# A decoder layer on one core: the second gate's modulation beside the output projection, and nine instead of seven FFN units with seven products

## The chip, the core and the metric

The kernel runs on one core of a Trainium2 chip. It is one program for one transformer layer. The metric is the device time of a whole execution in microseconds (us), as the median of several runs. The engines are named as in the profile: TensorE (PE) for matmuls, VectorE (DVE), ScalarE (ACT), GpSimd (POOL), and SyncE (SP), which here does nothing but issue DMAs. Each engine executes its own list of instructions in a fixed order and waits on semaphores for the others.

## What is computed

One layer over 256 rows (`x` is 1 x 256 x 2048, f32), with six modulation vectors made from a conditioning vector `c`:

```python
mod = silu(c) @ w_ada + b_ada
shift1, scale1, gate1, shift2, scale2, gate2 = split(mod, 6)
h = rms_norm(x, norm1_gain) * (1 + scale1) + shift1
x = x + gate1 * mixing_sublayer(h, ...)        # ends in "y @ w_out"
h = rms_norm(x, norm2_gain) * (1 + scale2) + shift2
x = x + gate2 * swiglu(h, w_ffn_in, w_ffn_out) # (silu(h@Wg) * (h@Wu)) @ w_ffn_out
```

`mixing_sublayer` is one projection `h @ w_in` whose columns feed three token mixers (stick-breaking attention, dilated attention, gated linear attention); their gated sum `y` is projected by `w_out` (2048 x 2048). The FFN is 5632 wide: `w_ffn_in` is 2048 x 11264, `w_ffn_out` 5632 x 2048. `w_ada` is 2048 x 12288, of which each of the six vectors takes 2048 columns.

## The kernel before

**Tiles.** The 256 rows are two tiles t of 128 (NT = 2). The 2048 rows of a weight are 16 chunks k of 128 (KC = 16), its columns are taken in blocks of 512 (NB). Every f32 product is made of three matmuls of a reduced f32 type (`mm3`, L164 to L166): high part by high part, low part of the weight by the high part of the data, high part of the weight by the low part of the data. A block of 512 columns is therefore 16 chunks x 2 tiles x 3 matmuls = 96 matmuls of 128 x 512.

**Weights.** `load_weights` fetches two chunks at a time, a "raw" of 512 KB, with a DMA from SP (L146). ScalarE casts a raw to its high part `whi` (L158), VectorE subtracts to get the low part `wlo` (L159); this is called a split below. A raw is 128 x 1024, the two chunks side by side. There are four rooms each for raw, whi and wlo, and some blocks take spare rooms besides. A raw is fetched when its room is free, so a split that is done late makes a DMA late.

**Stages.** The projections by `w_in` and the mixers run from 0 to about 760 us. Then comes the output projection, four blocks n = 0 to 3. `residual` (L1176, L1177) multiplies a block by gate1 and adds it to x, and ScalarE sums the squares. The last block is done for t = 0 first and for t = 1 afterwards from the same split weights, which stay in eight spare rooms, so that norm 2 of t = 0 runs beside the matmuls of t = 1.

**Norm 2.** `norm2_rows` waits for the sums of squares (L1183), works out the root and scales the 4 x 512 columns of a tile into `ada` (L1187, VectorE). `norm2_turn` transposes these 16 times on TensorE (L1199); ScalarE applies scale2 and shift2 to each 128 x 128 (L1206) and casts the high part H (L1210); VectorE makes the low part (L1211). FFN unit 0 is also done for t = 0 first; the second turn stands within its block for t = 0.

**FFN.** There are 11 units of 512 columns, each with a block for the gate half and one for the up half, then a turn of 8 transposes (L1122) into the layout of the output product. In the units listed in `FAST` three of the eight weight pairs are done by `fast_products` with seven products instead of eight, for which VectorE makes sums of weights (L1296 to L1326). The output product by `w_ffn_out` follows in two halves (`OUT_A`, `OUT_B`).

**Background.** The modulation vectors are made by background generators kept in `bg`. `tick(rate)`, called once for each weight pair of a block, lets them go on by that many steps. A step is a DMA of 512 KB of `w_ada` by SP into one of the rooms in `ring["tags"]` (L384), and, a few steps later, a multiply-and-add of 128 x 1024 on VectorE (L289), a "mac" below. `flush()` does all that remains. gate2 is made in units 8 to 10 and flushed in the output product.

**Order.** A scheduler sets the order of instructions on each engine when the program is built; `prio()` brings work forward, `issue_after` holds a DMA back until a given matmul. Buffers have tags (`A7`, `OS1`, `KD`...): two tiles with the same tag share one piece of memory, and the later one waits for the earlier one's readers.

Of the kernel before, what the change touches and what calls it, by code (L numbers as in the profile page):

```python
# [32 lines left out]
RATE_IN, RATE_MID, RATE_FFN = 0.8, 0.6, 0.65  # L33
RATE_OUT = 2.5
# [10 lines left out]
FAST = range(1, 8)  # L45
# [30 lines left out]
def trunk(ctx: ExitStack, tc: tile.TileContext, I, out):  # L76
# [91 lines left out]
    def block(pss, act, src, k0, k1, c0, base=0, w=None, tiles=range(NT), go_on=False, more=False, seeded=False,  # L168
              steps=None):
# [1022 lines left out]
    def norm2_turn(t, xs):  # L1192
# [8 lines left out]
        for j, ps in enumerate(banks):  # L1201
            hf = S(("KC", "T6")[j - 2], [P, 4, P]) if t == 0 and j >= 2 else scr([P, 4, P])
# [36 lines left out]
    w = load_weights(I["w_out"], 0, KC, 3 * NB, spare=("T0", "T3", "OS0", "OS1", "OS2", "OD", "A7", "A11"))  # L1239
    flush()  # L1240
    sh2, sc2 = mod2[SEG_SHIFT2], mod2[SEG_SCALE2]
    h2 = ([S(f"H{j}", [P, 4, T], F32R) for j in range(4)], [S(f"H{4 + j}", [P, 4, T], F32R) for j in range(4)])
    for t in range(NT):
        ps = acc_bank()
        block({t: ps}, y_at, None, 0, KC, 0, w=w, tiles=(t,), steps={N2_AT[0]: lambda: norm2_turn(0, xs)} if t else None)
# [5 lines left out]
    def h2_at(k, t):  # L1251
# [5 lines left out]
    ftags = ["A0", "A1", "A5", "A6", "A7", "A9", "A10", "A11", "A12", "T0", "T1", "T2", "T3", "T4", "T5",  # L1257
             "OS0", "OS1", "OS2", "OD", "KD", "H0", "H1"]
# [134 lines left out]
    def fast_unit(i):  # L1393
        own, other = (misc_bank, acc_bank) if i % 2 else (acc_bank, misc_bank)
        return fast_products(w_ff, i * NB, DFF + i * NB, PAIRS, h2_at, h2s, own, other, ("OD", "KD"))

    state["rate"] = RATE_FFN
    state["more_rooms"] = tuple(zip(X2_TAGS[0::2], X2_TAGS[1::2]))
    ring["tags"] = ("AR0", "AR1", "KC")
    act = []  # L1400
    for i in range(NFF):
        if i in FAST:
# [3 lines left out]
        if i == FAST[-1] + 1:  # L1406
            ring["tags"] = ("AR0", "AR1", "KC", "A2", "A3")
            bg.append(gate2_bg())
        if i in FAST:
            pass  # L1410
        elif i == 0:
            w = load_weights(w_ff, 0, KC, 0, spare=("A12", "KD", "A9", "A10", "A0", "A1", "T1", "T2"))
            for t in range(NT):
                block(pg, h2_at, None, 0, KC, 0, w=w, tiles=(t,), steps=None if t else {N2_AT[1]: lambda: norm2_turn(1, xs)})
# [150 lines left out]
```

## Time and profile before

| what | value |
|---|---|
| median of 3 runs | 1591.57 us (1590.14 to 1591.96) |
| profiled execution, its own time | 1590.96 us |
| its span, first to last instruction | 1589.2 us |
| PE busy | 1577.6 us (99%) |
| DVE busy | 1299.3 us (82%) |
| ACT busy | 852.6 us (54%) |
| data moved by DMA | 400.16 MB, mean 252 GB/s |
| granted TensorE clock, mean | 1.000 |

The span is 1.8 us shorter than the execution, which includes the start and end. A row of the timeline reads: start in us, duration in us, engine, line, operation, output <- input, shape, and, where the engine stood idle before, the length of that idle time and what ended it. Matmuls are pipelined: a 128 x 512 matmul is listed with 0.39 us, but the next one begins about 0.23 us after it, and it is this distance that counts. A row of the chain of waits gives start, duration and what it is. A row of the windows gives, for a stretch of time, each engine's busy time in us, the granted clock, the DMA share and the rate.

### The profile page before, as it was taken

The page shows a single profiled execution, that of the slowest core. Times are in us where ns is not written, and L with a number is a line of the kernel's source. Part 1 is how long each engine was busy: PE and PEld are TensorE (multiplying, and loading weights), DVE is VectorE, ACT ScalarE, POOL GpSimd, SP SyncE. Part 2 cuts the span into 40 slices and gives each one's busy share as a digit, 9 for nine tenths or more (in the row PEclk, how much of TensorE's full clock was granted, in tenths as well). Part 3 has the DMA queues.
Part 4 walks back from the last instruction along what each step waited for, and adds up shares of the span by engine and source line. Part 5 has one row for each costly group of instructions (what it writes and reads, how often), then busy time and mean ns, then how long its engine had stood idle before and what let it go on. Part 6 is the DMA issues. An engine that isn't in the chain of part 4 may idle for free.

```text
span 1589.2 us, 20174 instructions
## 1 busy us (share of the span) xinstructions
PE 1577.6 (99%) x7243; PEld 1304.6 (82%) x7243; DVE 1299.3 (82%) x1556; ACT 852.6 (54%) x1195; POOL 11.2 (1%) x22
## 2 busy tenths in 40 slices
PE   9999999999999999999999999999999999999998
PEld 7878888888888888888887888888888888888887
DVE  6889996888888686877756689999997677998884
ACT  5654448775764444444445756555554434455552
POOL 1000000000000000000000000000000000000000
PEclk9999999999999999999999999999999999999999
DMA  9999997677788899988767566666668789866664
GB/s 334 360 328 322 333 305 241 212 229 231 231 267 271 300 300 324 307 278 298 230 206 244 174 195 189 198 202 196 206 191 279 259 290 311 275 193 219 201 207 138
DMA packets 195740, 400.16 MB, mean 252 GB/s; under 512 B 13038, under 2 KB 28052, under 8 KB 195640
## 3 DMA queue, kind: packets, MB, share of 16 engines
q1 hardware_dynamic: 194664, 396.70, 75.9%
q0 software_dynamic: 800, 2.11, 0.3%
q8 instruction: 57, 0.93, 0.2%
q14 instruction: 43, 0.35, 0.1%
q10 hardware_dynamic: 176, 0.07, 0.0%
HBM read 394.63 MB, written 4.19 MB: 251 GB/s over the span
## 4 chain that ended last, share of the span: by engine, by line
PE 88%; DVE 4%; ACT 3%; DMA 3%; issue 2%; SPq 0%; ACTq 0%; DVEq 0%
PE acc L166 22%; PE acc L165 21%; PE acc L164 21%; PE misc L165 6%; PE misc L166 6%; PE misc L164 5%; DMA raw<-w_in 2%; PE acc L443 1%; ACT whi L158 1%; DVE wlo L159 1%; DMA raw<-w_br_gla 1%; DVE wlo L1309 1%; PE misc L812 1%; PE misc L1122 1%; ACT scr L638 1%
## 5 line engine op out<-in xcount | busy, mean ns | idle before, releaser
L158 ACT CAST whi<-raw 128x1024 fp32r<-128x1024 f32 x362 | 368.5, 1022 | 406.0 <-PE acc L166 270.2
L159 DVE TENSOR_TENSOR wlo<-raw,whi 128x1024 fp32r<-128x1024 f32 x362 | 425.6, 1183 | 186.8 <-ACT whi L158 184.8
L164 PE MATMUL acc<-whi,H 128*128 128x512 f32 x1245 | 487.3, 392 | 1.2 <-ACT H L455 0.8
L165 PE MATMUL acc<-wlo,H 128*128 128x512 f32 x1245 | 486.3, 391 | 0.8 <-DVE wlo L159 0.7
L166 PE MATMUL acc<-whi,H 128*128 128x512 f32 x1245 | 486.0, 391 | 0.4 <-DVE H L462 0.4
L166 PEld LDWEIGHTS acc<-whi,H 128*128 128x128 f32 x1245 | 233.6, 188 | 50.7 <-DVE H L462 1.6
L164 PEld LDWEIGHTS acc<-whi,H 128*128 128x128 f32 x1245 | 233.7, 188 | 50.0 <-ACT H L455 1.3
L165 PEld LDWEIGHTS acc<-wlo,H 128*128 128x128 f32 x1245 | 233.9, 188 | 48.6 <-DVE wlo L159 1.7
L1308 ACT CAST whi<-raw 128x1024 fp32r<-128x1024 f32 (+1 forms) x148 | 142.0, 974 | 100.4 <-PE acc L166 37.0
L1309 DVE TENSOR_TENSOR wlo<-raw,whi 128x1024 fp32r<-128x1024 f32 (+1 forms) x148 | 162.8, 1122 | 10.9 <-ACT whi L1308 9.5
L165 PE MATMUL acc<-wlo,A 128*128 128x512 f32 x222 | 86.5, 390 | 0.8 <-DVE wlo L159 0.8
L164 PE MATMUL acc<-whi,A 128*128 128x512 f32 x222 | 87.0, 392 | 0.0
L166 PE MATMUL acc<-whi,A 128*128 128x512 f32 x216 | 84.1, 389 | 0.0
L289 DVE SCALAR_TENSOR_TENSOR ada<-AR,csil,ada 128x1024 f32<-128x1024 f32 x51 | 64.8, 1278 | 1.8 <-DMA AR<-w_ada 1.6
L164 PE MATMUL misc<-whi,H 128*128 128x512 f32 x158 | 61.7, 391 | 0.0
L165 PE MATMUL misc<-wlo,H 128*128 128x512 f32 x158 | 61.6, 390 | 0.0
L166 PE MATMUL misc<-whi,H 128*128 128x512 f32 x158 | 61.5, 389 | 0.0
L165 PEld LDWEIGHTS acc<-wlo,A 128*128 128x128 f32 x222 | 41.7, 188 | 9.5 <-DVE wlo L159 1.1
L164 PEld LDWEIGHTS acc<-whi,A 128*128 128x128 f32 x222 | 41.7, 188 | 8.6 <-ACT whi L158 0.3
L1308 ACT CAST A<-raw 128x1024 fp32r<-128x1024 f32 (+1 forms) x36 | 34.9, 982 | 25.5 <-DMA raw<-w_ffn_in 9.1
L1308 ACT CAST whi<-AR 128x1024 fp32r<-128x1024 f32 x24 | 25.3, 1053 | 42.1 <-PE misc L166 20.6
L166 PEld LDWEIGHTS acc<-whi,A 128*128 128x128 f32 x216 | 40.6, 188 | 8.5
(487 smaller groups left out, 2306.3 us busy)
## 6 DMA issues: line engine op xcount, KB each, us to landing
raw<-w_in SPq DMA_DIRECT2D x205, 512.0 KB, 5.0
raw<-w_ffn_in SPq DMA_DIRECT2D x176, 512.0 KB, 4.6
raw<-w_ffn_out SPq DMA_DIRECT2D x88, 512.0 KB, 5.1
AR<-w_ada SPq DMA_DIRECT2D x70, 512.0 KB, 5.0
raw<-w_out SPq DMA_DIRECT2D x32, 512.0 KB, 4.8
KC<-w_ada SPq DMA_DIRECT2D x26, 512.0 KB, 5.3
OS<-w_ada SPq DMA_DIRECT2D x16, 512.0 KB, 6.5
KD<-w_ada SPq DMA_DIRECT2D x16, 512.0 KB, 5.5
```

Of the source, the lines that this page charges most:

```text
L158: state["cast"] = nc.scalar.copy(hi[:, :n, :], raw[:, :n, :])
L159: state["split"] = nc.vector.tensor_tensor(lo[:, :n, :], raw[:, :n, :], hi[:, :n, :].bitcast(F32), op=ALU.subtract)
L164: nc.tensor.matmul(ps, lh, rh, start=start, stop=False, skip_group_check=seeded)
L165: nc.tensor.matmul(ps, lh, rl, start=False, stop=False, skip_group_check=seeded)
L166: state["mm"] = nc.tensor.matmul(ps, ll, rh, start=False, stop=stop, skip_group_check=seeded)
L289: nc.vector.scalar_tensor_tensor(acc, raw, c, acc, op0=ALU.mult, op1=ALU.add)
L443: state["warm"] = nc.tensor.matmul(ps, ones_r, wide, start=True, stop=True)
L638: nc.scalar.activation(junk, heads(b)[:, t, h, :], AF.Square, accum_out=ss[:, t, i : i + 1])
L812: nc.tensor.matmul(ps[:n, t * N_GLA + h, :].rearrange("p (s l) -> p s l", l=L), at(f, h, t)[:, :n], odd(at(f, h, t)), start=True, stop=True,)
L1122: nc.tensor.transpose(ps[:, i, :], src[:, i * P : (i + 1) * P], ident)
L1308: nc.scalar.copy(hi[:, :n, :], src)
L1309: state["split"] = nc.vector.tensor_tensor(lo[:, :n, :], src, hi[:, :n, :].bitcast(F32), op=ALU.subtract)
```

## The change

The change has two parts that share the room for buffers.

*Fast units.* `FAST` is `range(2, 11)` instead of `range(1, 8)`: units 2 to 10 instead of 1 to 7. Unit 1 becomes a plain one, 8, 9 and 10 become fast ones. In unit 10 only one pair of the extra rooms (`more_rooms`) is used.

*Gate2.* Its background generator is started before the output projection instead of in unit 8, at a rate of 0.68 steps for each weight pair, with two accumulators of 128 x 1024 (tags OS0 and T3) and its own rooms for loads (A12, KD, KC, H7, later others). It runs beside the output projection and the first two FFN units, and what is left is flushed ahead of unit 2. `pace` multiplies the rate in the blocks done tile by tile: 0.5 for t = 0 of the last output block, 0 for t = 1 of it, 0 for t = 0 of unit 0 and 0.5 for t = 1. Then GpSimd's queue writes the two sums to DRAM (`gate2_away`), and SP fetches them again in the output product, at hook 7, where `flush` stood. shift2 and scale2 are no longer flushed ahead of norm 2 but ticked until scale2 is there. Some tags change: the spare rooms of the last output block, the places to which x2 is brought back, those of the activations of the last units, and which bank of sums a fast unit starts with.

In all, the changed program has 18 matmuls of 128 x 512 fewer on TensorE, 6 operations of 128 x 1024 and 46 of 128 x 512 more on VectorE, 14 more on ScalarE, and two more DMAs of 128 x 1024 each on POOL and SP.

The order of instructions moves at three places that matter. Lines of the changed kernel are one higher or lower: a split is L158, a mac L290, L1188 is the L1187 of before, L1200 the L1199.

First, SP's queue at the last block of the output projection. Before, its weights stand one after the other, followed by those of FFN unit 0:

```order
L146 DMA raw_7449<-w_out 128x2x512
L146 DMA raw_7455<-w_out 128x2x512
L146 DMA raw_7461<-w_out 128x2x512
L146 DMA raw_7467<-w_out 128x2x512
L146 DMA raw_7473<-w_out 128x2x512
L146 DMA raw_7677<-w_ffn_in 128x2x512
```

Now, with the fourth to eighth raw of the same block (raw_7501 is the fourth) and the steps of gate2:

```order
L145 DMA raw_7501<-w_out 128x2x512
L385 DMA A_1584_7361<-w_ada 128x1024
L385 DMA KD_7388<-w_ada 128x1024
L385 DMA KC_7403<-w_ada 128x1024
L145 DMA raw_7507<-w_out 128x2x512
L385 DMA H_1587_7430<-w_ada 128x1024
L145 DMA raw_7513<-w_out 128x2x512
L385 DMA A_1588_7445<-w_ada 128x1024
L145 DMA raw_7519<-w_out 128x2x512
L145 DMA raw_7525<-w_out 128x2x512
L145 DMA raw_7739<-w_ffn_in 128x2x512
```

Five loads of w_ada have come to stand among the raws; each waits until the mac that read its room last is done, and what is behind it on the queue waits too.

Second, VectorE from the residual of t = 0 in the last block (scr<-T,acc) to the first row of norm 2 (ada). Before:

```order
L1176 TENSOR_TENSOR scr_7536<-T_926_4162,acc_7487 128x512
L1177 TENSOR_TENSOR A_1476_6927<-A_1476_6927,scr_7536 128x512
L159 TENSOR_TENSOR wlo_7680<-raw_7677,whi_7679 128x1024
L1183 TENSOR_REDUCE tiny_7541<-x2ss 128x1
L257 TENSOR_SCALAR tiny_7543<-tiny_7541 128x1
L159 TENSOR_TENSOR wlo_7686<-raw_7683,whi_7685 128x1024
L159 TENSOR_TENSOR wlo_7692<-raw_7689,whi_7691 128x1024
L262 SCALAR_TENSOR_TENSOR tiny_7548<-tiny_7545,tiny_7543 128x1
L263 TENSOR_SCALAR tiny_7548<-tiny_7548 128x1
L159 TENSOR_TENSOR wlo_7698<-raw_7695,whi_7697 128x1024
L1187 TENSOR_SCALAR ada_7551<-A_1473_6921,tiny_7545,tiny_7548 128x512
```

Now, the same stretch, from its residual on:

```order
L1177 TENSOR_TENSOR scr_7598<-T_926_4162,acc_7539 128x512
L290 SCALAR_TENSOR_TENSOR T_1506_6982<-KC_7403,csil,T_1506_6982 128x1024
L1178 TENSOR_TENSOR A_1478_6929<-A_1478_6929,scr_7598 128x512
L158 TENSOR_TENSOR wlo_7748<-raw_7745,whi_7747 128x1024
L1184 TENSOR_REDUCE tiny_7603<-x2ss 128x1
L158 TENSOR_TENSOR wlo_7754<-raw_7751,whi_7753 128x1024
L258 TENSOR_SCALAR tiny_7605<-tiny_7603 128x1
L158 TENSOR_TENSOR wlo_7760<-raw_7757,whi_7759 128x1024
L290 SCALAR_TENSOR_TENSOR OS_1505_6981<-H_1587_7430,csil,OS_1505_6981 128x1024
L263 SCALAR_TENSOR_TENSOR tiny_7610<-tiny_7607,tiny_7605 128x1
L158 TENSOR_TENSOR A_1670_7766<-raw_7763,A_1669_7765 128x1024
L264 TENSOR_SCALAR tiny_7610<-tiny_7610 128x1
```

Behind these come a third mac (T_1506<-A_1588) and then the first L1188: three macs and four splits stand between, where before there were four splits alone.

Third, the two turns of norm 2. TensorE at the first turn, the transposes (misc<-ident,ada) among the matmuls of t = 1 (acc_7556 before). Before:

```order
L164 MATMUL acc_7556<-OS_1593_7469,A_1471_6917 128x512
L1199 MATMUL misc_7587<-ident,ada_7551 128x128 x4
L1199 MATMUL misc_7592<-ident,ada_7551 128x128 x4
L1199 MATMUL misc_7597<-ident,ada_7551 128x128 x4
L1199 MATMUL misc_7602<-ident,ada_7551 128x128 x4
L165 MATMUL acc_7556<-OD_7470,A_1471_6917 128x512
L166 MATMUL acc_7556<-OS_1593_7469,A_1472_6918 128x512
```

Now (acc_7618 is t = 1 of the last block, acc_7737 is unit 0, H its data):

```order
L165 MATMUL acc_7618<-A_1616_7527,A_1472_6918 128x512
L1200 MATMUL misc_7649<-ident,ada_7613 128x128 x4
L1200 MATMUL misc_7654<-ident,ada_7613 128x128 x4
L1200 MATMUL misc_7659<-ident,ada_7613 128x128 x4
L1200 MATMUL misc_7664<-ident,ada_7613 128x128 x4
L163 MATMUL acc_7737<-whi_7741,H_1618_7531 128x512
L164 MATMUL acc_7737<-wlo_7742,H_1618_7531 128x512
```

Before, 37 matmuls of t = 1 stood ahead of the transposes and 11 behind them; now all 48 stand ahead, eight of them among the last of t = 0, and the first product with H follows at once. In the second turn, the six matmuls of t = 0 that stood behind the transposes stand ahead of them too. On VectorE, two macs stand directly ahead of the second turn's L1188, where there was none:

```order
L1212 TENSOR_TENSOR H_1625_7538<-T_1645_7690,H_1621_7534 128x4x128
L158 TENSOR_TENSOR T_1679_7784<-raw_7781,T_1678_7783 128x1024
L263 SCALAR_TENSOR_TENSOR tiny_7727<-tiny_7724,tiny_7722 128x1
L290 SCALAR_TENSOR_TENSOR OS_1505_6981<-KC_7542,csil,OS_1505_6981 128x1024
L264 TENSOR_SCALAR tiny_7727<-tiny_7727 128x1
L290 SCALAR_TENSOR_TENSOR T_1506_6982<-A_1628_7563,csil,T_1506_6982 128x1024
L1188 TENSOR_SCALAR ada_7730<-A_1475_6923,tiny_7724,tiny_7727 128x512
```

The last low part of the first turn (H_1625) still comes ahead of them.

The diff, cut to what the text speaks of:

```diff
-RATE_IN, RATE_MID, RATE_FFN = 0.8, 0.6, 0.65
-RATE_OUT = 2.5
+RATE_IN, RATE_MID, RATE_LATE = 0.8, 0.6, 0.68
-FAST = range(1, 8)
+FAST = range(2, 11)
...
     def block(pss, act, src, k0, k1, c0, ..., steps=None, pace=None):
+        if pace is None:
+            pace = 1.0 if tiles[-1] == NT - 1 else 0.0
         for k in range(k0, k1):
-            if (k - k0) % 2 == 0 and tiles[-1] == NT - 1:
-                tick(state["rate"])
+            if (k - k0) % 2 == 0:
+                tick(state["rate"] * pace)
...
     def bring_back(n):
-        x2[n] = S(X2_TAGS[n], [P, NT, NB])
+        x2[n] = S(("OS1", "OS2", "OD", "KD")[n], [P, NT, NB])
         nc.sync.dma_start(x2[n], x2_away[n])
+    gate2_away = [away.tile([P, 2 * NB], F32, tag=f"gate2_{j}", name=nm("gate2")) for j in range(2)]
+    def gate2_bg():
+        acc = biased([S(tag, [P, 2 * NB]) for tag in ("OS0", "T3")], SEG_GATE2)
+        yield from ada_segment_steps(acc, SEG_GATE2, None, False)
+        yield from last_macs()
+        for j in range(2):
+            nc.gpsimd.dma_start(gate2_away[j], acc[j])
+    state["rate"] = RATE_LATE
+    ring["tags"] = ("A12", "KD", "KC", "H7")
+    bg.append(gate2_bg())
     for n in range(4):
...
-    w = load_weights(I["w_out"], 0, KC, 3 * NB, spare=("T0", "T3", "OS0", "OS1", "OS2", "OD", "A7", "A11"))
-    flush()
+    w = load_weights(I["w_out"], 0, KC, 3 * NB, spare=("T0", "AR0", "AR1", "OS1", "OS2", "OD", "A7", "A11"))
+    ring["tags"] = ("A12", "KD", "KC")
+    while SEG_SCALE2 not in mod2:
+        tick(1)
...
-        block({t: ps}, y_at, None, 0, KC, 0, w=w, tiles=(t,), steps=...)
+        block({t: ps}, y_at, None, 0, KC, 0, w=w, tiles=(t,), steps=..., pace=0 if t else 0.5)
...
-    def gate2_bg():
-        acc = state["gate2"] = biased(halves(S("ada", [P, D])), SEG_GATE2)
-        yield from ada_segment_steps(acc, SEG_GATE2, None, False)
-        yield from last_macs()
...
-    state["rate"] = RATE_FFN
-    ring["tags"] = ("AR0", "AR1", "KC")
+    ring["tags"] = ("A12", "KD", "KC", "T0")
     for i in range(NFF):
+        if i == FAST[0]:
+            flush()
+        if i == NFF - 1:
+            state["more_rooms"] = state["more_rooms"][:1]
...
-        if i == FAST[-1] + 1:
-            ring["tags"] = ("AR0", "AR1", "KC", "A2", "A3")
-            bg.append(gate2_bg())
...
-                block(pg, h2_at, None, 0, KC, 0, w=w, tiles=(t,), steps=...)
+                block(pg, h2_at, None, 0, KC, 0, w=w, tiles=(t,), steps=..., pace=0.5 * t)
...
-    state["rate"] = RATE_OUT
-    hooks[7] = flush
+    def gate2_back():
+        state["gate2"] = [S(tag, [P, 2 * NB]) for tag in ("A2", "A3")]
+        for j in range(2):
+            nc.sync.dma_start(state["gate2"][j], gate2_away[j])
+    hooks[7] = gate2_back
```

More of the change, by code (lines that the diff above doesn't have):

```diff
@@ L1201, in norm2_turn @@
         for j, ps in enumerate(banks):
-            hf = S(("KC", "T6")[j - 2], [P, 4, P]) if t == 0 and j >= 2 else scr([P, 4, P])
+            hf = S(("OD", "T6")[j - 2], [P, 4, P]) if t == 0 and j >= 2 else scr([P, 4, P])
             h2_raw[j, t] = hf
@@ L1433, in trunk, with turn @@
                 nc.vector.tensor_mul(sgs[t], sgs[t], pu[t])
-        def turn(sgs=sgs, hi=hi, lo=lo, bank=acc_bank if i + 1 in FAST and i % 2 == 0 else misc_bank):
+        def turn(sgs=sgs, hi=hi, lo=lo, bank=acc_bank if i % 2 else misc_bank):
             for t in range(NT):
```

33 lines of the change are left out of this document (19 added, 14 removed).

## The prediction

> **What bounds the kernel now.** I read the page's first part, then the chain of waits by engine, then windows cut along the stages, then single rows of the one stage where the tensor engine waits.
>
> ```profile
> PE 1577.6 (99%) x7243; PEld 1304.6 (82%) x7243; DVE 1299.3 (82%) x1556; ACT 852.6 (54%) x1195; POOL 11.2 (1%) x22
> PE 88%; DVE 4%; ACT 3%; DMA 3%; issue 2%; SPq 0%; ACTq 0%; DVEq 0%
> ```
>
> TensorE is busy in 99% of the span and carries 88% of the chain. Time is therefore matmuls issued plus the moments in which TensorE stands still. The windows show where it has no slack (first busy figure) and what VectorE and the DMAs have left (third busy figure, last two columns):
>
> ```profile
> core 0: us, PE busy (x) PEld busy (x) DVE busy (x) ACT busy (x) POOL busy (x), PEclk, DMA share, GB/s
> 100.00:150.00 50.00, 50.00 (x226) 41.52 (x225) 47.84 (x51) 19.15 (x19) 0.00 (x0) 1.00 0.97 339
> 800.00:850.00 50.00, 50.00 (x223) 41.39 (x221) 28.42 (x28) 23.38 (x28) 1.10 (x2) 1.00 0.67 212
> 860.00:890.00 30.00, 29.40 (x142) 23.12 (x141) 21.57 (x37) 23.40 (x52) 2.38 (x3) 1.00 0.54 178
> 866.00:870.00 4.00, 3.84 (x27) 3.06 (x25) 3.97 (x9) 1.56 (x3) 0.00 (x0) 1.00 0.92 304
> 950.00:1000.00 50.00, 50.00 (x226) 41.47 (x226) 47.32 (x59) 28.47 (x32) 0.00 (x0) 1.00 0.65 210
> 1250.00:1300.00 50.00, 50.00 (x226) 41.52 (x225) 38.90 (x36) 21.19 (x23) 0.00 (x0) 1.00 0.86 289
> ```
>
> 800 to 850 is the output projection, 860 to 890 holds norm 2 (866 to 870 its first turn), 950 to 1000 fast FFN units, 1250 to 1300 plain units with the gate2 work beside them. Only norm 2 leaves TensorE idle (29.40 of 30).
>
> **The change, part by part: fewer matmuls.** The unit turns (8 transposes each) mark the units on the chain:
>
> ```profile
> 1137.01 0.88 PE misc L1122 x8
> 1179.38 0.87 PE acc L1122 x8
> 1221.77 0.88 PE misc L1122 x8
> 1266.21 0.87 PE misc L1122 x8
> 1310.62 0.87 PE misc L1122 x8
> ```
>
> Fast units take 42.37 and 42.39 us, plain ones 44.44 and 44.41: 2.045 apart. A plain unit has 192 matmuls (2 halves, 2 tiles, 16 chunks, 3 products), so one costs (44.41 - 0.87)/192 = 0.2268 us, and 2.045 is the 9 matmuls that seven products save. Units 1 to 7 were fast, 2 to 10 are: two more, 18 matmuls, **-4.1 us**. VectorE's extra sums in units 8 to 10 are covered: a fast unit leaves VectorE at 47.32 of 50 with TensorE at 50.00, and the macs that stood in units 8 to 10 are gone. Unit 1 becomes plain with macs, as 1250 to 1300 (38.90 of 50). If that cover went, TensorE would wait for the split weights in every fast unit.
>
> **Macs beside the output projection.** Each gate2 step is a 512 KB load on SP's queue and one 128x1024 VectorE mac:
>
> ```profile
> 549.22 1.28 DVE L289 SCALAR_TENSOR_TENSOR T<-KC,csil,T 128x1024 f32<-128x1024 f32 x1
> 550.41 1.22 DVE L159 TENSOR_TENSOR wlo<-raw,whi 128x1024 fp32r<-128x1024 f32 x1
> 551.55 1.27 DVE L289 SCALAR_TENSOR_TENSOR T<-KD,csil,T 128x1024 f32<-128x1024 f32 x1
> DMA to landing us min/median/max: 3.8/6.6/9.4
> 572.81 0.50 PE L164 MATMUL acc<-whi,A 128*128 128x512 f32 x1
> 574.07 0.50 PE L165 MATMUL acc<-wlo,A 128*128 128x512 f32 x1 [0.76 <-DVE wlo L159]
> ```
>
> From start to start a mac costs 1.19 us, a split 1.14. VectorE has 21 us of 50 free at 800 to 850, and DMA has 339 - 212 = 127 GB/s of room, so the full blocks n = 0 to 2 I cost at nothing: hidden behind 50.00 of 50 TensorE. SP's order is the price. In the last block's t=0 the raws of its fifth to eighth weight pair now stand behind five w_ada loads, each of which waits for a mac to free its buffer; they leave some 3 to 4 us later than now. Nothing waits there today. Low end 0; high end 2.0, twice the 574.07 stall (1.26 from start to start, less 0.23, is 1.03), since four pairs can be late; I take **+1.2**, near the one such stall seen.
>
> **Norm 2, first turn.** Today:
>
> ```profile
> 848.64 0.39 PE L164 MATMUL acc<-whi,A 128*128 128x512 f32 x1
> 859.52 0.39 PE L164 MATMUL acc<-whi,A 128*128 128x512 f32 x1
> 859.72 0.69 DVE L1176 TENSOR_TENSOR scr<-T,acc 128x512 f32<-128x512 f32 x1 [2.38 <-PE acc L166]
> 860.44 0.69 DVE L1177 TENSOR_TENSOR A<-A,scr 128x512 f32<-128x512 f32 x1
> 863.35 0.15 DVE L1183 TENSOR_REDUCE tiny<-x2ss 128x1 f32<-128x4 f32 x1
> 863.77 2.39 DVE L159 TENSOR_TENSOR wlo<-raw,whi 128x1024 fp32r<-128x1024 f32 x2
> 867.54 1.91 DVE L1187 TENSOR_SCALAR ada<-A,tiny,tiny 128x512 f32<-128x512 f32 x4
> 868.23 2.00 PE L1199 MATMUL misc<-ident,ada 128*128 128x128 f32 x16 [0.16 <-DVE ada L1187]
> 870.66 1.86 ACT L1206 ACTIVATE scr<-misc,mod,mod 128x128 f32<-128x128 f32 x5
> 872.38 0.39 PE L166 MATMUL acc<-A,A 128*128 128x512 f32 x1
> 872.38 0.64 ACT L1210 CAST H<-scr 128x512 fp32r<-128x512 f32 x1
> 873.07 0.50 PE L164 MATMUL acc<-whi,H 128*128 128x512 f32 x1 [0.30 <-ACT H L1210]
> ```
>
> t=0 ends at 859.52. VectorE starts the residual 0.20 later, the transposes come at 868.23, after 37 matmuls of t=1, and 11 more t=1 matmuls cover ScalarE's scale and cast; TensorE loses 873.07 - 872.38 - 0.23 = 0.46. In the changed order, VectorE has between the same residual and L1188 (L1187 today) three macs and four splits. Back to back: the residual's two 0.72 + 0.60, macs 3 x 1.19, splits 4 x 1.14, four small ones 0.15 each, the first row to the transposes 0.69 as today: 10.7, with the start 10.9 us after t=0. TensorE has 40 t=1 matmuls left (8 went ahead among those of t=0): 40 x 0.2268 = 9.1. So it waits 1.8, or 1.6 more than the 0.16 of today, if nothing in this row is late. Today the same row without the macs takes 867.54 - 859.72 = 7.8 us where its pieces sum to 6.5, so 1.3 of it is waiting for weights; with that the cost is 2.9. I take **+2.6**, near today's behaviour. The transposes now stand directly ahead of the first h2 matmul, so the scale and cast have no cover.
>
> **Second turn and the casts.** Today:
>
> ```profile
> 882.70 1.92 DVE L1187 TENSOR_SCALAR ada<-A,tiny,tiny 128x512 f32<-128x512 f32 x4
> 882.78 0.39 PE L166 MATMUL acc<-A,H 128*128 128x512 f32 x1
> 883.30 2.03 PE L1199 MATMUL misc<-ident,ada 128*128 128x128 f32 x16
> 885.09 0.48 PE L164 MATMUL acc<-T,H 128*128 128x512 f32 x1
> 885.72 0.64 ACT L1210 CAST H<-scr 128x512 fp32r<-128x512 f32 x1
> 886.55 0.40 PE L164 MATMUL acc<-whi,H 128*128 128x512 f32 x1
> ```
>
> Six matmuls from 885.09 hide the cast that ends at 886.36; without them TensorE would wait 886.36 - 885.09 = 1.27. Both turns lose that cover. First turn: 1.27 less the 0.46 paid today, 0.8 to 1.4 (a weight cast ahead of it on ScalarE), **+1.0**. Second turn: **+1.2**, 1.0 to 1.3. Two macs now also stand ahead of the second L1188: from the first turn's L1206 to this row are 882.70 - 870.66 = 12.0 us today, 14.4 with 2 x 1.19, plus 0.6 to the transposes; TensorE has until then 1.1 + 1.27 + 48 x 0.2268 = 13.3 us from the same point. The wait could be 1.7, against 0.29 today; part of the macs falls into idle stretches of VectorE, so net 0 to 1.4, **+0.5**.
>
> **The rest at nothing.** The sums' way to DRAM and back (four 512 KB transfers, landing in under 10 us against hundreds of us of slack), ScalarE's 14 more operations (23.4 of 30 is its fullest window here), bank parity and tags: hidden by TensorE's 50.00 of 50.
>
> **Sum.** -4.1 + 1.2 + 2.6 + 1.0 + 1.2 + 0.5 = **+2.4 us**; low ends -4.1 + 0 + 1.6 + 0.8 + 1.0 + 0 = -0.7, high ends -4.1 + 2.0 + 2.9 + 1.4 + 1.3 + 1.4 = +4.9. The profiled execution took 1590.96 (span 1589.2), 0.6 under the median 1591.57; the sum on it is 1593.4, on the median **1594.0**, which I predict.
>
> **A rule against the change.** The granted clock is 1.00 in every window above, and the longest wait quoted is 1.03 us. After the change, 2.6 + 0.16 of waiting, 16 transposes of 1.75 in all and a cast wait of 1.3 follow one another: 5.8 us without a plain matmul. The Trainium skill, "TensorE: Matmul & The Clock Gate", states in Part 1 that the clock falls to half after one idle window of about 3.4 us and needs as long again of work to come back, and in Part 4 that transposes do not count as work in the same way. No window of this trace tests it. By it a falling clock is likely here, and the sum would be that of the third rival; by the trace's 1.00 the sum stands.
>
> **Rivals.** *The turns stay covered* (faster): if VectorE takes the macs early, in idle time such as the 2.38 ahead of 859.72, and the casts come early too, only the matmuls count: 1591.57 - 4.1 = 1587.5. It decides when the new waits stay below 0.9 us (3.2, the bound below, of the 4.1). Against it: the 1.6 comes from bare durations in a fixed order. Chance 0.12. *Weights land late at norm 2* (slower): the last split ahead of L1188 needs a raw whose buffer is freed by a split just before t=0's end, and VectorE comes to it some 8 us later. A cast costs 1.05, so a landing above 6.9 adds one to one; the 9.4 maximum adds 2.5 on the first turn, and I set 1 for the second: +5.9, 1597.5. It decides from a landing of 7.7, where the sum passes 0.2%. For it: 866 to 870 moves 304 GB/s already without w_ada. Against it: the median is 6.6 where macs and weights shared the queue. Chance 0.13. *The clock falls* (slower): after the long wait the 16 transposes (1.75) and the first weight pair's six matmuls on t=0 (6 x 0.227 = 1.36) run at half speed and cost as much again, 3.1: +5.5, 1597.1. By the Trainium skill's time to come back, in the same Part 1, the price would be an estimated 3.4. It decides once more than 0.8 us is lost so. For it: no gap like it stands in the trace. Against it: 1.00 through all the waits that do. Chance 0.09.
>
> **How the numbers follow.** 0.2%, or 3.2 us, is about what a measurement of this kernel tells from no change: 1588.4 to 1594.75. My case has the remaining 0.66: of its -0.7 to +4.9 around +2.4 about 0.7 lies within 0.2%, 0.46, and the rest above, 0.20. Slower 0.20 + 0.13 + 0.09 = 0.42, same 0.46, faster 0.12. The range leaves out most of the faster case and the far end of the late one: 1590.0 to 1598.0.
>
> **What would show it.** Right: unit turns 42.4 apart through unit 10; the transposes of norm 2 waiting for L1188 by 2 to 3 us, H waits of 1 us behind both; from the last block's first matmul to the first h2 matmul of t=1 some 44 us, where 848.64 to 886.55 took 37.9. Wrong: that stretch at 38 or 39 us (first rival), landings over 7.7 there (second), or a granted clock below 1.00 (third); also any new wait in units 8 to 10 or at the end, where I put none.

## The result, and the profile after

The changed kernel takes 1599.07 us (median of 4 runs, 1597.32 to 1600.14) against 1590.86 us (1589.28 to 1591.96) for the kernel before: 1.0051 times as long, 95% interval 1.0034 to 1.0069. It is 8.2 us slower, where 1594.0 had been forecast, and above the range of 1590.0 to 1598.0. The profiled execution took 1600.14 us, its span is 1598.4 us, 9.2 more than the span before.

The page of the kernel after, its engines and its chain of waits by engine:

```profile
PE 1578.4 (99%) x7225; PEld 1302.8 (82%) x7225; DVE 1330.4 (83%) x1608; ACT 861.5 (54%) x1209; POOL 12.3 (1%) x24
PE 86%; DVE 5%; DMA 5%; ACT 2%; issue 1%; SPq 0%; ACTq 0%; DVEq 0%
```

TensorE has 18 instructions fewer, but the chain leaves it in 14% of the span where it was 12%. The windows say where (columns as before: busy time of the engines, the granted clock, then DMA):

```profile
800.00:850.00 50.00, 50.00 (x222) 41.41 (x221) 39.45 (x39) 21.56 (x26) 1.10 (x2) 1.00 0.88 302
840.00:860.00 20.00, 19.02 (x83) 15.09 (x82) 16.88 (x18) 9.14 (x12) 0.53 (x1) 1.00 0.97 338
860.00:890.00 30.00, 26.35 (x118) 21.03 (x117) 25.99 (x39) 17.59 (x36) 0.53 (x1) 0.94 0.84 289
950.00:1000.00 50.00, 48.42 (x218) 39.84 (x217) 38.16 (x43) 22.19 (x25) 1.06 (x2) 1.00 0.64 216
1250.00:1300.00 50.00, 50.00 (x226) 41.50 (x225) 45.84 (x55) 30.67 (x35) 0.00 (x0) 1.00 0.59 193
1400.00:1450.00 50.00, 47.47 (x200) 38.21 (x200) 39.56 (x44) 26.79 (x29) 0.00 (x0) 0.97 0.53 169
```

Four stretches lose time: the last output block and norm 2 (840 to 890), FFN unit 2 (950 to 1010), and the start of the output product (1400 to 1450). In two of them the granted clock is below 1.00. The fast units behave as forecast. Their turns on the chain:

```profile
1063.50 1.01 PE acc L1123 x8
1106.02 0.87 PE misc L1123 x8
1148.39 0.87 PE acc L1123 x8
1190.79 0.88 PE misc L1123 x8
1233.18 0.87 PE acc L1123 x8
...
1360.34 0.88 PE misc L1123 x8
```

They stand 42.4 us apart to the end. Norm 2, on the timeline:

```profile
847.39 0.39 PE L163 MATMUL acc<-whi,A 128*128 128x512 f32 x1
855.88 0.50 PE L164 MATMUL acc<-OS,T 128*128 128x512 f32 x1 [0.76 <-DVE OS L158]
862.52 0.68 DVE L1177 TENSOR_TENSOR scr<-T,acc 128x512 f32<-128x512 f32 x1
870.52 0.39 PE L165 MATMUL acc<-A,A 128*128 128x512 f32 x1
872.16 1.91 DVE L1188 TENSOR_SCALAR ada<-A,tiny,tiny 128x512 f32<-128x512 f32 x4
872.85 2.00 PE L1200 MATMUL misc<-ident,ada 128*128 128x128 f32 x16 [1.95 <-DVE ada L1188]
876.55 0.50 PE L163 MATMUL acc<-whi,H 128*128 128x512 f32 x1 [1.71 <-ACT H L1211]
879.57 0.63 PE L163 MATMUL acc<-whi,H 128*128 128x512 f32 x1
879.99 0.63 PE L164 MATMUL acc<-wlo,H 128*128 128x512 f32 x1
892.51 0.50 PE L163 MATMUL acc<-whi,H 128*128 128x512 f32 x1 [1.14 <-ACT H L1211]
```

The order of the forecast is there: the transposes wait for L1188, and both turns wait for the cast. From 879.57 to 879.99 a matmul takes 0.43 us instead of 0.23: the clock has been halved. The start of the output product:

```profile
1415.66 0.69 DVE L1324 TENSOR_TENSOR AR<-raw,raw 128x512 f32<-128x512 f32 x1 [3.04 <-DMA raw<-w_ffn_out]
1416.27 3.49 DVE L1321 TENSOR_TENSOR wlo<-raw,whi 128x1024 fp32r<-128x1024 f32 x3
1417.54 0.69 PE L164 MATMUL acc<-wlo,T 128*128 128x512 f32 x1 [2.33 <-DVE wlo L1321]
```

VectorE waits 3.04 us for a raw that only a sum (L1324) needs, and three splits that TensorE needs stand behind it. Then matmuls run at 0.43 us until 1421. In the kernel before, at this stage, the three splits came first and the sum behind them:

```profile
1406.80 3.50 DVE L1309 TENSOR_TENSOR wlo<-raw,whi 128x1024 fp32r<-128x1024 f32 x3
1410.21 0.69 DVE L1312 TENSOR_TENSOR AR<-raw,raw 128x512 f32<-128x512 f32 x1
```

In unit 2 it is the same picture: a sum waits 3.52 us for its raw, with the low part of unit 1's activations (L193) behind it. The raw is late because it left late: SP could send for it only when the sum at 977.19 had freed its room, and a mac of the flush stands directly ahead of that sum.

```profile
975.99 1.28 DVE L290 SCALAR_TENSOR_TENSOR T<-A,csil,T 128x1024 f32<-128x1024 f32 x1
977.19 0.68 DVE L1324 TENSOR_TENSOR KD<-raw,KD 128x512 f32<-128x512 f32 x1
977.90 0.37 SPq L1308 DMA_DIRECT2D raw<-w_ffn_in  x1
984.41 0.69 DVE L1324 TENSOR_TENSOR OD<-raw,raw 128x512 f32<-128x512 f32 x1 [3.52 <-DMA raw<-w_ffn_in]
986.23 0.68 DVE L193 TENSOR_TENSOR A<-acc,A 128x512 fp32r<-128x512 f32 x1
986.97 0.50 PE L163 MATMUL acc<-A,AR 128*128 128x512 f32 x1 [1.58 <-DVE A L193]
```

TensorE's losses, each the distance of two starts less 0.227 us (the distance of two matmuls without a wait), account for the difference of the two profiled executions:

| where | us |
|---|---|
| 18 matmuls | -4.1 |
| last output block, t=0 | +1.4 |
| first transposes of norm 2 (2.1, before 0.3) | +1.8 |
| waits for the casts (1.75 and 1.19, before 0.46 and 0) | +2.5 |
| second transposes (0, before 0.3) | -0.3 |
| first half clock, 8 matmuls by 0.20 | +1.6 |
| unit 2 (1.74 and 0.73) | +2.5 |
| output product (0.37 and 2.49) | +2.9 |
| second half clock, 8 matmuls by 0.20 | +1.6 |
| a wait at 1484 of the kernel before | -0.55 |
| sum | +9.35, measured 9.2 |

### The profile page after: what moved, and what is told of

Read it like the earlier page. It is cut to its first block, busy times and chain, and to the rows that moved or that the text cites. A ratio compares the mean times of both kernels' runs of the same rounds, so it can differ in the third digit from the quotient of the medians.

```text
span 1598.4 us, 20213 instructions
## 1 busy us (share of the span) xinstructions
PE 1578.4 (99%) x7225; PEld 1302.8 (82%) x7225; DVE 1330.4 (83%) x1608; ACT 861.5 (54%) x1209; POOL 12.3 (1%) x24
## 4 chain that ended last, share of the span: by engine, by line
PE 86%; DVE 5%; DMA 5%; ACT 2%; issue 1%; SPq 0%; ACTq 0%; DVEq 0%
PE acc L165 21%; PE acc L164 21%; PE acc L163 21%; PE misc L163 6%; PE misc L164 6%; PE misc L165 6%; DMA raw<-w_ffn_in 2%; DVE wlo L158 1%; DVE wlo L1321 1%; DMA raw<-w_ffn_out 1%; DVE T L290 1%; PE acc L444 1%; PE misc L813 1%; PE misc L1123 1%; DMA A<-x 0%
## 5 line engine op out<-in xcount | busy, mean ns | idle before, releaser
L157 ACT CAST whi<-raw 128x1024 fp32r<-128x1024 f32 x330 | 334.7, 1019 | 358.4 <-PE acc L165 212.5
L158 DVE TENSOR_TENSOR wlo<-raw,whi 128x1024 fp32r<-128x1024 f32 x330 | 386.3, 1179 | 147.3 <-ACT whi L157 145.1
L163 PE MATMUL acc<-whi,H 128*128 128x512 f32 x1141 | 447.3, 393 | 3.7 <-ACT H L1211 2.8
L164 PE MATMUL acc<-wlo,H 128*128 128x512 f32 x1141 | 446.5, 391 | 0.8 <-DVE wlo L158 0.7
L165 PE MATMUL acc<-whi,H 128*128 128x512 f32 x1141 | 446.1, 392 | 0.4 <-DVE H L463 0.4
L163 PEld LDWEIGHTS acc<-whi,H 128*128 128x128 f32 x1141 | 214.5, 188 | 48.7 <-ACT H L1211 3.3
L165 PEld LDWEIGHTS acc<-whi,H 128*128 128x128 f32 x1141 | 214.5, 188 | 46.7 <-DVE H L463 1.6
L164 PEld LDWEIGHTS acc<-wlo,H 128*128 128x128 f32 x1141 | 214.7, 188 | 44.8 <-DVE wlo L158 1.7
L1320 ACT CAST whi<-raw 128x1024 fp32r<-128x1024 f32 (+1 forms) x169 | 161.5, 971 | 111.4 <-PE acc L165 41.7
L1321 DVE TENSOR_TENSOR wlo<-raw,whi 128x1024 fp32r<-128x1024 f32 (+1 forms) x169 | 184.6, 1117 | 15.0 <-ACT whi L1320 13.9
L163 PE MATMUL misc<-whi,H 128*128 128x512 f32 x193 | 75.6, 391 | 0.6 <-DVE misc L1355 0.6
L165 PE MATMUL misc<-whi,H 128*128 128x512 f32 x193 | 75.2, 389 | 0.0
L1321 DVE TENSOR_TENSOR A<-raw,A 128x1024 fp32r<-128x1024 f32 (+1 forms) x47 | 52.9, 1139 | 4.4 <-ACT A L1320 4.4
L290 DVE SCALAR_TENSOR_TENSOR ada<-AR,csil,ada 128x1024 f32<-128x1024 f32 x39 | 49.4, 1278 | 3.3 <-DMA AR<-w_ada 3.3
```

The source lines that it names most:

```text
L157: state["cast"] = nc.scalar.copy(hi[:, :n, :], raw[:, :n, :])
L158: state["split"] = nc.vector.tensor_tensor(lo[:, :n, :], raw[:, :n, :], hi[:, :n, :].bitcast(F32), op=ALU.subtract)
L163: nc.tensor.matmul(ps, lh, rh, start=start, stop=False, skip_group_check=seeded)
L164: nc.tensor.matmul(ps, lh, rl, start=False, stop=False, skip_group_check=seeded)
L165: state["mm"] = nc.tensor.matmul(ps, ll, rh, start=False, stop=stop, skip_group_check=seeded)
L290: nc.vector.scalar_tensor_tensor(acc, raw, c, acc, op0=ALU.mult, op1=ALU.add)
```

## The experiments

Theory 1: the gate2 loads and macs cause all losses up to unit 2. Theory 2: the output product's wait comes either of the fast unit 10 ahead of it (2a) or of the order on VectorE, sums ahead of splits (2b).

**No macs.** `gate2_bg` without its steps, so the kernel leaves out gate2's matrix product:

```diff
-        yield from ada_segment_steps(acc, SEG_GATE2, None, False)
```

> The changed kernel without the 32 loads and macs of gate2 (its matrix product is left out, gate2 is its bias alone; the two sums still go to DRAM and back). In the changed kernel's profile TensorE loses 1.4 us in the last block's t=0, about 3.7 at norm 2's two turns, 2 by a clock that falls behind them, 2.7 in FFN unit 2 and 4.9 at the start of the output product. Theory 1 (the macs cause everything but the last): 1599.1 - 1.4 - 3.7 - 2 - 2.7 = about 1589, with the output product's wait of 2 to 3 us at the same place and its half clock behind it. Rival (the order around norm 2 was lost to the moved tags and rooms, not to macs): 1595 or more, transposes of norm 2 still without cover. Second rival (the macs cause the output product's wait too): about 1585.

1590.95 us, ratio to before 1.0007 (0.9998 to 1.0017). The transposes are back among the matmuls of t=1:

```profile
867.58 2.00 PE L1200 MATMUL misc<-ident,ada 128*128 128x128 f32 x16 [0.16 <-DVE ada L1188]
872.86 0.50 PE L163 MATMUL acc<-whi,H 128*128 128x512 f32 x1 [0.77 <-ACT H L1211]
```

Unit 2 loses nothing (TensorE 50.00 of 50 from 950 to 1000), the clock is 1.00 there and at norm 2, and the output product's waits of 1.06, 0.37 and 2.26 are still there. Theory 1 holds, and the moved tags alone do no harm at norm 2. The time is 2 us above its forecast, as a wait of 1.5 in unit 10 came in addition.

**Seven fast units.**

```diff
-FAST = range(2, 11)
+FAST = range(2, 9)
```

> The changed kernel with units 2 to 8 fast, 9 and 10 plain: as many matmuls as before the change, so 4.1 us more than the changed kernel by matmuls alone. Theory 2a (the wait at the start of the output product comes of a fast unit 10 standing right ahead of it): the wait goes, 1599.1 + 4.1 - 4.9 = 1598.3. Theory 2b (it comes of the order on VectorE, sums of the next fast pair ahead of splits, which stands in this kernel too): the wait stays, 1603.2.

1601.8 us, ratio 1.0068 (1.0053 to 1.0083). With a plain unit 10 ahead of it the output product still waits:

```profile
1421.31 0.50 PE L164 MATMUL acc<-wlo,T 128*128 128x512 f32 x1 [1.56 <-DVE wlo L1321]
```

Its waits at the start of the output product sum to 2.8 us (0.75, 0.37, 1.72), as in the changed kernel: theory 2a is out. It is 2.7 us over the changed kernel where 18 matmuls are 4.1; unit 2 lost 1.3 instead of 2.5.

**No macs at norm 2.**

```diff
-RATE_IN, RATE_MID, RATE_LATE = 0.8, 0.6, 0.68
+RATE_IN, RATE_MID, RATE_LATE = 0.8, 0.6, 0.8
...
-              pace=0 if t else 0.5)
+              pace=0)
...
-                block(pg, h2_at, ..., pace=0.5 * t)
+                block(pg, h2_at, ..., pace=0)
```

> The changed kernel with a pace of 0 in all four split blocks and a rate of 0.8 instead of 0.68, so that all macs stand in the three whole output blocks, unit 0's up half and unit 1, and none at norm 2 and little in the flush ahead of unit 2. Theory 1: the waits at norm 2 go back to those of before, no clock falls there, unit 2 has no wait: 1599.1 - 1.4 - 3 - 2 - 2.7 = about 1590, with the wait in the output product left. Rival (more loads for each weight pair starve the output projection): waits of several us between 780 and 850 us, 1594 or more.

1607.5 us, ratio 1.0105 (1.0088 to 1.0122): a miss of 17 us. TensorE loses 5.1 us in the last output block, and 5.1 at one place in unit 0:

```profile
921.76 1.28 DVE L290 SCALAR_TENSOR_TENSOR OS<-H,csil,OS 128x1024 f32<-128x1024 f32 x1
922.95 1.28 DVE L290 SCALAR_TENSOR_TENSOR T<-A,csil,T 128x1024 f32<-128x1024 f32 x1
924.15 0.68 DVE L1212 TENSOR_TENSOR H<-T,H 128x512 fp32r<-128x512 f32 x1
...
924.88 0.80 PE L165 MATMUL acc<-T,H 128*128 128x512 f32 x1 [4.95 <-DVE H L1212]
```

The mac at 921.76 reads a load that lies in H7, the tile into which norm 2 writes its low part. With the pace at 0 that mac is put off, and norm 2 with it.

**H7 not a room for loads.** The last kernel with

```diff
-    ring["tags"] = ("A12", "KD", "KC", "H7")
+    ring["tags"] = ("A12", "KD", "KC")
```

> The kernel without macs at norm 2 of before, at rate 0.8 (1607.5 us), with H7 taken out of the rooms for loads and nothing else. Theory (the 5.1 us wait in unit 0 is norm 2's low part waiting to be written to H7, which still holds a load whose mac is not done): that wait goes, the second turn gets its cover back, about 1600, and 5 us of waits stay in the last output block, where loads stand ahead of raws. Rival (a mac ahead of the low part on VectorE): the wait stays, 1607.

1596.76 us in one run. The wait at 924 is gone, and the second transposes have their cover again; the last block still loses 6.2 us (0.66, 2.04, 2.96, 0.51). So for unit 0 the theory holds: norm 2's low part waited for H7.

**Loads away from the last block.** H7 not a room, the pace 0 in all split blocks, rate 0.8, and none in the second half of block n=2; with the sums held (below) and without:

```diff
-        block(pss, y_at, I["w_out"], 0, KC, n * NB)
+        block(pss, y_at, I["w_out"], 0, KC, n * NB, pace=(1,) * 4 + (0,) * 4 if n == 2 else None)
```

> The changed kernel with four edits: no steps of gate2 in the four split blocks and in the second half of block n=2, so that no load of w_ada stands among the last block's raws; H7 not among the rooms for loads (norm 2 writes H7); rate 0.8; and the sums of the output product held behind the preceding split. If macs and loads near norm 2 and the order of sums are the whole of the loss, the transposes stand 11 and 6 matmuls ahead of the block's end again, and the time is 1599.1 - 1.4 (last block) - 3.7 (norm 2) - 2 (clock) - 1.5 (part of unit 2) - 3 (as measured for the sums) = about 1587.5, below the kernel before. Rival (the macs cannot be put anywhere without a wait: loads at 0.8 starve the blocks 0 to 2 or units 0 and 1): 1592 or more, with waits of TensorE for splits between 780 and 970 us.

> The same without the edit of the sums in the output product. Theory: the parts add, 3 us more than with it, about 1590.5, with the wait of 2 to 2.5 us near the start of the output product. Rival (the wait there depends on when the kernel arrives): no such wait, 1587.5.

1594.33 us, ratio 1.0026 (1.0018 to 1.0035), and 1599.26 us, ratio 1.0053 (1.0037 to 1.0068). The parts add (4.9 us between the two). Norm 2 loses what it lost before the change, 1.0 us in all, but the last block loses 3.4, as VectorE and ScalarE wait for raws, and unit 2 still loses 1.9 (0.85 and 1.05). A window of the first of the two, and its timeline:

```profile
830.00:840.00 10.00, 10.00 (x46) 8.29 (x45) 6.18 (x6) 3.78 (x5) 0.54 (x1) 1.00 0.99 344
```

```profile
852.67 1.04 ACT L157 CAST T<-raw 128x1024 fp32r<-128x1024 f32 x1 [3.43 <-DMA raw<-w_out]
853.76 0.50 PE L163 MATMUL acc<-T,T 128*128 128x512 f32 x1 [1.42 <-ACT T L157]
```

At 830 to 840 the DMA queues are full, share 0.99 at 344 GB/s, and raws sent for from 838 to 856 land in 7.5 us (median), where those from 840 to 880 of the kernel before took 4.8. The loads asked for earlier push the raws back. The rival was right.

**Splits first.** In the output product, the first two sums of a fast pair are held behind the last split of the pair ahead:

```diff
             r0, r1 = raw_at(c0), raw_at(c1)
+            ahead = state.get("split") if src is I["w_ffn_out"] else None
...
-            sub(ta[:, 0], r1[:, 0], r0[:, 0])
-            sub(ta[:, 1], r1[:, 1], r1[:, 0])
+            with tc.issue_after(ahead.ins) if ahead is not None else nullcontext():
+                sub(ta[:, 0], r1[:, 0], r0[:, 0])
+                sub(ta[:, 1], r1[:, 1], r1[:, 0])
```

> The changed kernel; in the output product the first two sums of a fast pair are held behind the split that precedes the pair, so that VectorE no longer waits for a sum's raw with ready splits behind it. Theory 2b: the wait of 2.5 us near 1415, the smaller one near 1404 and the half clock behind go, 1599.1 - 4.9 = 1594.2. Rival (the raws themselves are late, whatever stands ahead): VectorE waits at the split instead, the stall is the same, 1599.

1596.04 us, ratio 1.0031 (1.0018 to 1.0043), 3.0 below the changed kernel. On VectorE the three splits now come first, and TensorE waits nowhere in the output product:

```profile
1409.86 3.50 DVE L1321 TENSOR_TENSOR wlo<-raw,whi 128x1024 fp32r<-128x1024 f32 x3
1413.27 0.68 DVE L1324 TENSOR_TENSOR AR<-raw,raw 128x512 f32<-128x512 f32 x1
```

Theory 2b holds. It does not show what brought the order about, which stood in the kernels without macs and with a plain unit 10 too.

**The kernel before, gate2 done sooner.** Nothing of the change, only

```diff
-RATE_IN, RATE_MID, RATE_FFN = 0.8, 0.6, 0.65
+RATE_IN, RATE_MID, RATE_FFN = 0.8, 0.6, 0.9
```

so that no macs are left for the output product; and the same with the sums held.

> The kernel before, with one number changed: gate2's steps at a rate of 0.9 instead of 0.65 in units 8 to 10, so that all its loads and macs are done before the output product and none is left for it. Nothing of the change is in it. Theory (with no macs in the output product the scheduler sets the sums of a fast pair ahead of ready splits, and this order alone is the change's wait there): a wait of TensorE of 2 to 3 us some 10 to 20 us into the output product, 1590.8 + 3 = about 1594. Rival (the wait belongs to the change's tags and rooms, or to a fast unit 10): no such wait, 1590 to 1591.

> The same with the first two sums of a fast pair held behind the preceding split. Theory: the wait of the kernel with rate 0.9 goes, about 1591. Rival: 1594, the wait is at the split.

1602.63 us, ratio 1.0077 (1.0062 to 1.0092), and 1597.4 us, ratio 1.0042 (1.0027 to 1.0058). The first has no mac in the output product, where the kernel before had six from 1360 to 1371, and it has the changed kernel's wait to a tenth:

```profile
1422.17 0.69 DVE L1312 TENSOR_TENSOR AR<-raw,raw 128x512 f32<-128x512 f32 x1 [3.01 <-DMA raw<-w_ffn_out]
1422.78 3.49 DVE L1309 TENSOR_TENSOR wlo<-raw,whi 128x1024 fp32r<-128x1024 f32 x3
1424.05 0.50 PE L165 MATMUL acc<-wlo,T 128*128 128x512 f32 x1 [2.29 <-DVE wlo L1309]
```

Held sums take it away, 5.2 us in all. So it is enough that gate2's loads and macs are gone from the output product: the scheduler then puts sums ahead of splits, without the change's tags, rooms or fast units. By what rule it does so, no run shows. Both kernels are slower than forecast for another reason: the rate of 0.9 costs up to 6 us of waits near 1336 in the plain units, and a half clock behind them.

**What the units are worth.** No macs, and the sums held:

> The changed kernel without the loads and macs of gate2 (left out as before, gate2 is its bias alone) and with the sums of the output product held behind the preceding split. It shows what the two more fast units are worth when gate2 costs nothing. Theory (18 matmuls, 4.1 us, and nothing else is gained): 1590.2 - 4.1 = 1586, at most 2 us more for small waits. Rival (nine fast units in a row have waits of their own): 1590, with waits in units 8 to 10.

The edits are those of the first kernel and of the held sums together. 1586.21 us, ratio 0.9967 (0.9955 to 0.9978): 4.7 us below the kernel with macs left out and sums not held, and 5.1 below the kernel before, run beside it at 1591.34. The kernel leaves out gate2's product but the 18 matmuls are real and nothing in units 8 to 10 takes them back. What a complete kernel can win is this, less what 32 loads and macs cost.

**Attempts at a faster kernel.** Fast units 3 to 10, no steps in block n=2, rate 0.8 beside blocks n=0 and 1, then 0.62; sums held, H7 free, pace 0 in the split blocks; unit 2 takes the banks that a fast unit 2 would:

```diff
-FAST = range(2, 11)
+FAST = range(3, 11)
...
+            state["rate"] = 0.62
             block(pu, h2_at, w_ff, 0, KC, DFF + i * NB)
```

> The changed kernel with fast units 3 to 10 only, so that the macs have units 0, 1 and 2; no steps of gate2 in block n=2, the last block or unit 0's gate half; rate 0.8 in the blocks n=0 and 1 and 0.62 behind; H7 not among the rooms for loads; the sums of the output product held behind the preceding split. One fast unit more than before the change: 2.05 us fewer. Theory (the waits come of loads that saturate the DMA queues in the output projection, of macs at norm 2 and of macs in a fast unit, and none of these is left): 1590.2 - 2 = about 1588, the only one to beat the kernel before. Rival (11 us of loads in the blocks n=0 and 1 are enough to make the last block late): 1590 or more, with a wait near 852.

1590.84 us against 1591.34 run beside it, ratio 1.0002 (0.9993 to 1.0011): the same. The gain of the theory did not come, and neither did its rival's wait near 852 (0.36 us). Its only large wait is 1.71 us at 1345, where a split with a late raw stands ahead of unit 10's sums. Holding the first splits of the output product behind those sums, for two pairs, as shown here, and in a later kernel for one pair (`not ws` in place of `len(ws) < 2`) and behind the first half's sum alone:

```diff
-                add(o[1][half], u[:, 1 - half])
+                state["merged"] = add(o[1][half], u[:, 1 - half])
...
+                state["first"] = src is w_fo and len(ws) < 2 and c0 == 0
...
+            with tc.issue_after(state["merged"].ins) if state.get("first") else nullcontext():
+                state["split"] = nc.vector.tensor_tensor(...)
```

> The kernel with three plain units of before (1590.84 us), with the splits of the output product's first two weight pairs held on VectorE behind unit 10's last sum of products. In that kernel TensorE lost 1.7 us at 1345, when VectorE waited for a late raw of the output product with unit 10's sums behind it. Theory (it is again the fixed order): that wait goes, about 1589, one to two us below the kernel before. Rival (the output product's first splits then come too late themselves): a wait of the same size 5 to 10 us later, 1590.8.

> The kernel with three plain units (1590.84 us), with only the output product's first weight pair held on VectorE, and only behind the first half of unit 10's last sums. Theory (the wait at 1345 comes of one split ahead of two sums): the wait goes and none comes in the output product, about 1589, one to two us below the kernel before. Rival (the raws of the output product land late, and whatever stands behind them waits): 1591 to 1593, with a wait between 1345 and 1360.

Two pairs: 1593.66 us, ratio 1.0017 (1.0008 to 1.0026); the wait moved to the output product's first weights (2.9 us at 1352). One pair: 1590.68 us, ratio 0.9999 (0.9990 to 1.0008); the wait at 1345 is gone, but this profile lost 3.2 us near 852, where the kernel with the same order there had lost 0.4. With `FAST = range(2, 11)`, two pairs held and rate 0.9, or with three plain units, one pair held and 0.66 in place of 0.8:

> The same with units 2 to 10 fast, as in the change, and a rate of 0.9 so that the macs fit into the blocks n=0 and 1 and units 0 and 1. 2 us fewer matmuls than the kernel with three plain units. Theory (VectorE and the DMA queues have no room for 32 steps in two plain units and two blocks: some macs fall into unit 2, whose VectorE is full): waits of 1 to 3 us in unit 2 and near 852, 1590 to 1593. Rival (they fit): 1587.

> The kernel with three plain units and one pair held (1590.68 us), at a rate of 0.66 instead of 0.8 in the output projection's blocks n=0 and 1. Its profile had 3.2 us of waits near 852, where the loads of w_ada had pushed the raws of the last block back. Theory (fewer loads there, none late): waits near 852 below 0.5 us, about 1588.5. Rival (what is taken away there stands in unit 3 instead, or the waits near 852 come and go from execution to execution): 1590.5.

1595.74 us, ratio 1.0033 (1.0020 to 1.0045), above the 1590 to 1593 of its theory: 3.5 us near 852 to 861 and 2.6 in unit 2, where VectorE is full:

```profile
990.00:1010.00 20.00, 19.17 (x84) 15.21 (x83) 19.39 (x23) 11.64 (x13) 0.53 (x1) 1.00 0.73 236
```

And 1592.46 us, ratio 1.0010 (1.0001 to 1.0019): the rival. 1.6 us were still lost at 853, and 2.2 in unit 3, where macs now stand ahead of its first sums. None of the complete kernels beats the one before.

## Why the prediction was wrong

**The matmuls, -4.1.** Right: turns 42.4 us apart, and 5.1 us gained where gate2 costs nothing, one more than the matmuls; of that one, 0.55 is the wait at 1484 of the kernel before, and the rest is open.

**The last block, +1.2.** Right: 1.4, of which 1.03 is the size of the one stall it was priced by. The cause is more than the order on SP's queue: the DMAs are full (338 GB/s, share 0.97), and taking the loads out from among the raws, but asking for them sooner, did not help (3.4).

**Norm 2, +2.6, +1.0, +1.2, +0.5.** Right in mechanism, a little high: 1.8, 1.3, 1.2 and -0.3. The bare sum of VectorE's pieces (10.7 us to the transposes) met 872.85 - 862.52 = 10.3; the 1.3 us of waiting that I added from the kernel before did not come. The second turn's macs fell into VectorE's idle time. From 847.39 to 892.51 the stretch took 45.1 us, forecast 44; 1.6 of it is the clock.

**"The rest at nothing" and "the macs that stood in units 8 to 10 are gone".** This is the step that failed. The prediction priced the macs only where they went. Where they left, the output product, their absence changed the order of VectorE's other work, and that cost 2.9 us of waits and 1.6 of clock. The order there, sums ahead of splits, stands in the built program before any run; the prediction weighed the order at norm 2 and the last block only. The claim that VectorE's work "is covered" in the fast units also had a hole: the flush ahead of unit 2 leaves three macs among its first splits and sums (967.16, 970.06, 975.99), and that cost 2.5 us. It is not that VectorE was full: it was busy 38.16 us of 50 there. The macs made a raw leave late, and VectorE waited for it; without the loads and macs the loss is gone.

**The third rival, the clock.** It came true in the profiled execution, twice, at 1.6 us each where I had put 3.1 once; I gave it 0.09. The Trainium skill, "TensorE: Matmul & The Clock Gate", Part 1, speaks of an idle window of about 3.4 us. The traces have a window of that length, 3.413 us, but some 2.0 us of standing still within it were enough (the last section). The measurement decides. The rival's price was too high for one fall: half speed lasts 3.41 us and 8 matmuls, each 0.20 longer, so about half of that time is lost. The 3.4 that the prediction estimates by the skill's time to come back is the length of the stretch and not its cost.

**The second rival,** late landings, did not happen. For the raws from 840 to 880 the view of the tile gives:

```profile
DMA to landing us min/median/max: 4.5/6.0/7.2
```

All are under its 7.7. **The first rival,** covered turns, is refuted by the waits.

In sum: up to norm 2 the forecast of +6.5 met 5.4 (1.4 + 1.8 + 2.5 - 0.3); 7.0 of unit 2, output product and its clock, and 1.6 of the first clock, had been put at nothing. Without the two half clocks the profiled execution would lie 6.0 us above the one before, still 3.6 over the forecast of 2.4.

## What to carry to other kernels

Work that is moved away leaves a hole, and a scheduler with a fixed order fills it: compare the order of instructions where work was taken out, not only where it went, and look for an operation with a late input ahead of ready ones on an engine. Background work has a price that depends on the stage's last free resource: here VectorE in the fast units, the DMA queues in the output projection, and the order at norm 2. With units 2 to 10 fast and the sums held, the 32 steps cost about 10 us (1596.04 and 1595.74 against 1586.21 without them), more than twice the 4.1 of the 18 matmuls they were moved for. On an engine at 99%, a wait of two microseconds may cost another 1.6 through the clock.

## What the runs showed of the hardware

The granted clock fell only in some executions of the same kernel. Of the kernel with sums held, six runs were taken: at a mean clock of 1.000, 1592.9 to 1595.2 us (three runs); at 0.998 and 0.999, 1596.9 to 1597.2 (three). Its profiled execution, at 1592.88, had waits of 1.98 and 1.13 us at the first turn of norm 2, where the changed kernel had 2.1 and 1.75, and stayed at full clock.

The traces show what decides. In each of them the granted clock changes only on a raster of 3.413 us. In the changed kernel half speed begins at 878.38, 1.8 us after TensorE went on at norm 2, and at 1417.68, 0.1 us after it went on in the output product: the two are 158 steps of the raster apart, and both times half speed lasts one step. What counts is how long TensorE stands still within one step. In the changed kernel the wait of 2.49 us ahead of 1417.54 lies whole in one step, and the next step is at 0.50:

```profile
1414.27:1417.68 3.41, 1.08 (x6) 0.58 (x5) 2.02 (x3) 1.67 (x2) 0.00 (x0) 1.00 0.06 23
1417.68:1421.09 3.41, 3.41 (x9) 2.63 (x10) 3.41 (x5) 0.00 (x0) 0.00 (x0) 0.50 0.62 182
1421.09:1424.51 3.42, 3.42 (x17) 2.82 (x16) 2.39 (x3) 1.05 (x1) 0.00 (x0) 1.00 0.76 229
```

In the kernel with the loads away and the sums not held, a wait of 2.32 us at the same work is cut in two by the border at 1417.38, and the clock stays:

```profile
1413.97:1417.38 3.41, 2.48 (x11) 1.70 (x10) 0.66 (x2) 2.60 (x3) 0.00 (x0) 1.00 0.24 89
1417.38:1420.79 3.41, 2.19 (x10) 1.82 (x11) 3.41 (x5) 0.00 (x0) 0.00 (x0) 1.00 0.29 79
1420.79:1424.21 3.42, 3.42 (x17) 2.84 (x16) 3.38 (x6) 1.07 (x2) 0.00 (x0) 1.00 0.74 246
```

I summed for each step at full clock, in all the traces and without the start and the end of the kernels, the time that TensorE's matmuls (0.227 us each, a transpose 0.11) leave free. A step with 2.1 us or more of it was followed by half speed in all 12 cases. A step with 1.95 or less was so in one case alone, at 33.1 us of the kernel with seven fast units, where eight matmuls of one column (0.9 us in all) are counted as work. Between these, one with 2.01 was (norm 2 of the changed kernel) and one with 2.03 was not (norm 2 of the kernel with sums held), so the border lies near 2.0 us. The 16 transposes, which the prediction did not count as plain work, kept the clock up: the step from 871.55 to 874.96 of the changed kernel holds them and no other matmul, and full clock followed. By these traces, then, the same wait costs 1.6 us or nothing as the raster happens to cut it.

The waits near 852 also differ between executions with the same order (0.4 and 3.2 us). From 820 to 840 the DMA queues of these two move 331 and 327 GB/s, and raws sent for from 825 to 860 land in 4.2 to 7.9 and in 3.9 to 8.4 us. In the kernel before, at 244 GB/s from 840 to 860, those from 840 to 880 land in 4.6 to 5.9. So near full queues the landing of a single raw is no longer a fixed time.
